# From mixing to the second feed-forward: token tiles in groups of four, norms of two tiles at once, no GpSimd

## The chip, the cores and the metric

The kernel runs on one core of a Trainium2 chip. The metric is the time of one execution on the device in microseconds (us); lower is better. Five engines work beside each other, each through its own queue in order: TensorE (PE) multiplies and transposes into the eight banks of PSUM, VectorE (DVE), ScalarE (ACT) and GpSimd (POOL) compute between SBUF and PSUM, and SyncE (SP) issues the DMAs. The engines wait for each other by semaphores.

## What is computed

One decoder layer on 1024 tokens of width 1024, fp32. A SwiGLU feed-forward, a mixing stage (sliding-window attention beside a diagonal state-space model), and a second SwiGLU feed-forward, each with a norm ahead and a norm behind, and with a shift, a scale and a gate from a conditioning vector:

```python
x = x + 0.5 * ga1 * rms_norm(swiglu(modulate(rms_norm(x, g_pre_ff1), sh1, sc1), ...), g_post_ff1)
h = modulate(rms_norm(x, g_pre_mix), sh2, sc2)
attn, ssm = sliding_window_attention(...), s5_ssm(...)     # both from h @ w_in
# the end of s5_ssm: y * sigmoid(y @ w_glu + b_glu)
mixed = concatenate([rms_norm(attn, g_attn_out), rms_norm(ssm, g_ssm_out)]) @ w_out
x = x + ga2 * rms_norm(mixed, g_post_mix)
h = modulate(rms_norm(x, g_pre_ff2), sh3, sc3)
x = x + 0.5 * ga3 * rms_norm((silu(h @ w2_gate) * (h @ w2_up)) @ w2_down, g_post_ff2)
```

The stage that is changed is the end of the second half: the GLU, the half of `mixed` that comes from `ssm`, the two norms around `x + ga2 * ...`, the modulation, and the first products of the second feed-forward.

## The kernel before

Each fp32 operand of a product is held as two halves: `split` (L68) lets ACT cast the high part (L69) and DVE or POOL subtract it to get the low part (L70). A product is three matmuls (`mm3`, L72): high by high (L74), high by low (L75), low by high (L76). Tokens are taken in eight tiles of 128. The feed-forwards use a scheme of Strassen's kind on halves of the tokens and of the width; `GateUp` holds its activations in eight buffers `q0` to `q7`, one for each 128 columns of the width, each with all 1024 tokens, and `Weights` its weights, whose raw halves are loaded into the buffers `r0` to `r3` of 512 KB.

Code is written in program order and a scheduler (the Tile framework) sets the order of each engine's queue from it; a buffer is named by its tag (`a14`, `c0`, `b6`), and whoever takes a tag again waits until its last readers are done. `b0` to `b7` are the PSUM banks.

The end of `mix`, by lines: the GLU (L1012 to L1030) makes the state-space half and adds up its squares (`sqs`, the add at L1030 on POOL). Then a loop runs over the token tiles t. It multiplies the tile by the lower half of `w_out` into two banks; for t = 0 it also sums the squares over the columns by eight matmuls with ones (L1054). DVE adds the banks, scaled, to `acc[t]` (L1058), which holds the attention's half. `epilogue` (L249) loads the tile's residual x, takes the squares' sum (ACT L156), multiplies by the gate (L254, here on POOL), forms 1/rms by a short chain of operations on 128x1 (L141 to L145, L151), adds the residual (DVE L255), stores x, takes the squares' sum again and normalises (ACT L259). `turn(t)`, called three tiles later, calls `to_hf` (L210): four transposes (L205) go into a bank, four more into a second one, and the blocks of 128x128 are scaled and shifted one at a time into the `q` buffers, four by ACT (L222) and four by DVE (L226). As soon as tiles 0 to 3 stand in `q0` to `q3`, `g2.block` splits these into operands and `g2.first` starts the gate and up products. `wt.first` splits the first raw weights; POOL forms the low part of four of these, and of two of the operands.

Of the eight `acc` tiles, those of tiles 0 to 2 lie in `r1` to `r3`, the others in `a14`, `a15`, `a4`, `a5`, `a6`. Earlier, at the end of the attention, `late` loads and splits the GLU weights by way of `r0` and `c0`.

## Time and profile before

| | us |
|---|---|
| runs | 1713.24, 1706.69, 1712.78 |
| median | 1712.78 |
| the profiled execution, its own time | 1704.67 |
| its span in the trace | 1702.9 |
| PE busy in it | 1649.9 |
| the stage in question (GLU to the first gate and up products) | about 970 to 1115 |

The profile is one execution, and the times of all rows are from it. "Busy" is the time in which an engine executes; matmuls overlap a little, so their durations add up to more than the time between their starts, and the distance from start to start is the one to count with. The bracket at the end of a row of a timeline gives how long the engine stood idle before it, and what the trace takes for the cause: engine, buffer and line of the last thing it waited for. Names are those of the buffers without their numbers: `a<-r,a` is an operation that reads buffers `r` and `a` and writes an `a`. The granted clock is the share of TensorE's full speed.

### The profile page before, as it was taken

To read this page: it belongs to the slowest core of one execution; us is meant where nothing else is said; L and a number is where in the kernel's file an instruction comes from. 1 tells how busy PE (TensorE), PEld (TensorE's weight loads), DVE (VectorE), ACT (ScalarE), POOL (GpSimd) and SP (SyncE) were. 2 spreads that over 40 slices of the span, in tenths; PEclk is the share of its full clock that TensorE was granted. 3 is DMA by queue.
4 is the path that set the end of the run, shared out by engine and by line. 5 is a ranking of instruction groups with operands and counts; after the bars stand their busy time and mean duration, and the time that the engine had idled before them with its cause. 6 is when DMAs were issued, how large, how long until landed. Compare 5 with 4: busy or idle time off the path is not lost.

```text
span 1702.9 us, 22218 instructions
## 1 busy us (share of the span) xinstructions
PE 1649.9 (97%) x7669; PEld 1353.3 (79%) x7669; DVE 1264.4 (74%) x2470; ACT 803.6 (47%) x1654; POOL 120.7 (7%) x147
## 2 busy tenths in 40 slices
PE   6999999999999999899989998999999999999998
PEld 5888888787788878788767886878888888888886
DVE  7999988789779878735589368777666566678586
ACT  5633333553344557736564257633333333444462
POOL 0011100001100000000014053000000000000001
PEclk8999999999999999999999998999999999999999
DMA  9186742234495733410233126253322223493324
GB/s 382 40 284 232 257 163 94 105 135 148 137 355 189 231 121 136 163 36 15 90 97 87 50 81 200 75 201 106 117 94 93 93 101 123 158 377 114 112 97 163
DMA packets 112066, 249.08 MB, mean 146 GB/s; under 512 B 12089, under 2 KB 27745, under 8 KB 111953
## 3 DMA queue, kind: packets, MB, share of 16 engines
q1 hardware_dynamic: 102224, 214.12, 36.6%
q0 software_dynamic: 9152, 32.49, 5.7%
q8 instruction: 60, 0.98, 0.2%
q10 hardware_dynamic: 576, 1.05, 0.2%
q14 instruction: 54, 0.43, 0.1%
HBM read 187.87 MB, written 59.75 MB: 145 GB/s over the span
## 4 chain that ended last, share of the span: by engine, by line
PE 50%; DVE 5%; ACT 2%; DMA 1%; issue 1%; SPq 0%; POOL 0%; DVEq 0%; ACTq 0%; POOLq 0%
PE b L76 15%; PE b L75 15%; PE b L74 15%; PE b L751 1%; PE b L839 1%; PE b L841 1%; DVE a L70 1%; PE b L840 1%; PE b L930 1%; PE b L785 1%; PE b L926 1%; ACT a L69 0%; PE b L205 0%; DMA r<-in_w_gu 0%; DMA w<-in_w_out 0%
## 5 line engine op out<-in xcount | busy, mean ns | idle before, releaser
L75 PE MATMUL b<-a,w 128*128 128x512 f32 x1260 | 493.5, 392 | 5.0 <-DVE a L70 5.0
L74 PE MATMUL b<-a,w 128*128 128x512 f32 x1260 | 489.2, 393 | 8.6 <-ACT w L69 3.5
L76 PE MATMUL b<-a,w 128*128 128x512 f32 x1260 | 494.2, 392 | 3.2 <-DVE w L70 3.1
L74 PEld LDWEIGHTS b<-a,w 128*128 128x128 f32 x1260 | 238.0, 189 | 61.6 <-ACT w L69 3.9
L76 PEld LDWEIGHTS b<-a,w 128*128 128x128 f32 x1260 | 238.3, 189 | 55.6 <-DVE w L70 5.9
L75 PEld LDWEIGHTS b<-a,w 128*128 128x128 f32 x1260 | 238.2, 189 | 55.1 <-DVE a L70 6.1
L70 DVE TENSOR_TENSOR w<-r,w 128x512 fp32r<-128x512 f32 (+1 forms) x206 | 142.9, 694 | 128.6 <-ACT w L69 128.3
L75 PE MATMUL b<-w,r 128*128 128x512 f32 x528 | 205.5, 389 | 1.7 <-DVE w L70 1.7
L76 PE MATMUL b<-w,r 128*128 128x512 f32 x528 | 205.4, 389 | 0.0
L74 PE MATMUL b<-w,r 128*128 128x512 f32 x528 | 180.7, 389 | 0.0
L69 ACT CAST w<-r 128x512 fp32r<-128x512 f32 (+1 forms) x210 | 130.2, 623 | 91.8 <-DVE r L334 82.1
L69 ACT CAST r<-a 128x512 fp32r<-128x512 f32 x110 | 68.5, 623 | 148.9 <-PE b L76 112.0
L70 DVE TENSOR_TENSOR r<-a,r 128x512 fp32r<-128x512 f32 x110 | 75.7, 688 | 60.3 <-ACT r L69 59.9
L75 PEld LDWEIGHTS b<-w,r 128*128 128x128 f32 x528 | 99.1, 188 | 22.7 <-DVE w L70 2.1
L76 PEld LDWEIGHTS b<-w,r 128*128 128x128 f32 x528 | 99.1, 188 | 20.6
L74 PEld LDWEIGHTS b<-w,r 128*128 128x128 f32 x528 | 99.1, 188 | 20.5
L69 ACT CAST w<-t 128x512 fp32r<-128x512 f32 (+1 forms) x114 | 69.9, 613 | 87.4 <-DVE t L337 33.5
L70 DVE TENSOR_TENSOR w<-t,w 128x512 fp32r<-128x512 f32 (+1 forms) x114 | 79.7, 699 | 32.4 <-ACT w L69 32.1
L466 DVE TENSOR_TENSOR h<-h,b 128x512 f32<-128x512 f32 x120 | 82.1, 685 | 20.4 <-PE b L76 18.6
L454 ACT ACTIVATE h<-h 128x512 f32<-128x512 f32 x60 | 38.0, 633 | 117.8 <-DVE h L466 117.8
L70 DVE TENSOR_TENSOR w<-a,w 128x512 fp32r<-128x512 f32 x110 | 75.4, 685 | 0.4 <-ACT w L69 0.4
L74 PE MATMUL b<-a,a 128*128 128x512 f32 x182 | 72.0, 398 | 0.0
(376 smaller groups left out, 2548.2 us busy)
## 6 DMA issues: line engine op xcount, KB each, us to landing
r<-in_w_gu SPq DMA_DIRECT2D x88, 512.0 KB, 4.1
g_d<-h SPq DMA_DIRECT2D x154, 256.0 KB, 2.2
a<-g_d SPq DMA_DIRECT2D x110, 256.0 KB, 3.4
q<-in_w_ada POOLq DMA_DIRECT2D x48, 512.0 KB, 4.6
a<-in_w_d SPq DMA_DIRECT2D x88, 256.0 KB, 5.4
a<-in_w_ada SPq DMA_DIRECT2D x16, 512.0 KB, 10.1
a<-in_x SPq DMA_DIRECT2D x12, 512.0 KB, 5.9
x_d<-a SPq DMA_DIRECT2D x12, 512.0 KB, 3.8
```

The lines of the kernel that those rows point to most:

```text
L69: act.copy(hi, src)
L70: eng.tensor_tensor(lo, src, hi.bitcast(F32), op=SUB)
L74: pe.matmul(psum, wh, xh, start=first, stop=False, skip_group_check=goes_on)
L75: pe.matmul(psum, wh, xl, start=False, stop=False, skip_group_check=goes_on)
L76: pe.matmul(psum, wl, xh, start=False, stop=last, skip_group_check=goes_on)
L454: act.activation(dst, src, AF.Silu)
L466: dve.tensor_tensor(dst, dst, pb, op=ADD)
L751: pe.matmul(pb[kv][:, m % 2, ks], qT[m][rows, t * P : (t + 1) * P], kT[rows, (t + 1 - nk) * P : (t + 1) * P], start=True, stop=True,)
L785: pe.transpose(pt[:, m, :], pr[4 * kv + m][:, b * P : (b + 1) * P], ident)
L839: pe.matmul(pb, hh, wh, start=k == 0, stop=False)
L840: pe.matmul(pb, hh, wl, start=False, stop=False)
L841: pe.matmul(pb, hl, wh, start=False, stop=k == NK - 1)
```

## The change

In words, in the order of the diff:

- `GateUp.first` is cut up, so that the products of one operand block can be called alone (`first_part`).
- Two of the GLU's raw weights are loaded into `a9` instead of `c0`, and `acc[4]` lies in `c0` instead of `a15`.
- The squares are added up by DVE. The low parts of weights and operands are formed by DVE as well, and so is the gate multiply. POOL computes nothing in this stage.
- The loop over tiles becomes three functions. `share(t)` multiplies, adds to `acc[t]`, lets ACT sum the squares in two halves and DVE multiply by the gate in place. `joined(p)` does the norms of tiles 2p and 2p + 1: one chain on 128x2 for both, the residuals, the stores, the squares, a second chain, the normalised tiles. `turn(c, k)` transposes columns k of the four tiles of group c into one bank and lets ACT scale and shift the whole bank, 128x512, at once.
- Their order is written out: three shares, pair 0, two shares, pair 1, two shares, pair 2, group 0 with its operands, the loads of the raw weights, share 7, the rest of group 0, pair 3, and group 1 between the products.
- Residuals are loaded into four buffers instead of two.

```diff
+        def first_part(self, r, c, k, us):
+            x = self.A[f"a{r + 1}{c + 1}"][k]
+            for u in us:
+                for f in range(2):
...
+                    w = self.wt.ops[u, f, c][:, :, k * P : (k + 1) * P]
+                    mm3(self.pb[r, u, f], w[:, 0], w[:, 1], x[:, 0], x[:, 1], c == 0 and k == 0, c == 1 and k == 3)
...
+                self.first_part(r, c, k, (0, 1))
...
-        return Stream(ins, Rot(*names("r", 2, 3, 0, 1)), 3), Stream(us, Rot("w2", "w3"), 1), Stream(late, Rot("a14", "a15", "a14", "a15", "r0", "c0", "r0", "c0"), 1), Stream(shares, Rot(*names("w", 0, 1, 2, 3)), 3)
+        return Stream(ins, Rot(*names("r", 2, 3, 0, 1)), 3), Stream(us, Rot("w2", "w3"), 1), Stream(late, Rot("a14", "a15", "a14", "a15", "r0", "a9", "r0", "a9"), 1), Stream(shares, Rot(*names("w", 0, 1, 2, 3)), 3)
...
-            acc.append(slot(("r1", "r2", "r3", "a14", "a15", "a4", "a5", "a6")[t], [D]))
+            acc.append(slot(("r1", "r2", "r3", "a14", "c0", "a4", "a5", "a6")[t], [D]))
...
-                    pool.tensor_tensor(sqs[:, tk], sqs[:, tk], s2, op=ADD)
+                    dve.tensor_tensor(sqs[:, tk], sqs[:, tk], s2, op=ADD)
...
-        x_rot = Rot("a10", "a11")
...
-        def turn(t):
-            to_hf(t, acc[t], hf, 2, 2)
...
-        for t in range(NT):
...
+        def share(t):
...
-            epilogue(1, t, acc[t], grow, x_rot(), "a13", ("c0", "a8")[t % 2], True, pool)
-            if t >= 3:
-                turn(t - 3)
-            if t == 3:
...
-                    wt.load(u, 0)
-            if t == 5:
...
-                    wt.load(u, 1)
-                wt.first(0)
-            if t >= 6:
-                for k in range(3) if t == 6 else (3,):
-                    g2.block(0, 0, k)
+            X[t] = slot(("a10", "a11", "a13", "a8")[t % 4], [D])
+            sp.dma_start(X[t], x_d[1][t])
...
+            for dh, (dk, pb) in enumerate(zip(halves, pbs)):
+                f = acc[t][:, dk]
+                dve.scalar_tensor_tensor(f, pb, rstd_s[:, t : t + 1], f, op0=MUL, op1=ADD)
+                i = 2 * dh + t % 2
+                act.activation(slot(j_rot(), [512]), f, AF.Square, accum_out=ss[:, i : i + 1])
+            dve.tensor_tensor(acc[t], acc[t], grow, op=MUL)
...
+        def joined(p):
...
+            ss, sn = S[p]
+            dve.tensor_tensor(ss[:, 0:2], ss[:, 0:2], ss[:, 2:4], op=ADD)
+            r = rstd_of(ss[:, 0:2], 2, D)
+            for i in range(2):
+                t = 2 * p + i
+                dve.scalar_tensor_tensor(X[t], acc[t], r[:, i : i + 1], X[t], op0=MUL, op1=ADD)
+                sp.dma_start(x_d[2][t], X[t])
+                act.activation(acc[t], X[t], AF.Square, accum_out=sn[:, i : i + 1])
+            r = rstd_of(sn, 2, D)
+            for i in range(2):
+                t = 2 * p + i
+                act.activation(acc[t], X[t], AF.Identity, scale=r[:, i : i + 1])
...
+        def turn(c, k):
...
+            pt = bank(tr_rot(), [4, P])
+            for i in range(4):
+                pe.transpose(pt[:, i, :], acc[4 * c + i][:, k * P : (k + 1) * P], ident)
+            act.activation(
+                g2.q(c, k // 4, k % 4), pt.rearrange("p t q -> p (t q)"), AF.Identity,
+                scale=gsc[:, 2, k : k + 1], bias=mod(6)[:, k : k + 1],
+            )
...
+        for t in range(4):
+            share(t)
+            if t == 2:
+                joined(0)
+        share(4)
+        joined(1)
+        share(5)
+        share(6)
+        joined(2)
+        for k in range(4):
+            turn(0, k)
+            g2.block(0, 0, k)
+        for c in range(2):
+            for u in range(2):
+                wt.load(u, c)
+        wt.first(0)
+        share(7)
+        for k in range(4, 8):
+            turn(0, k)
...
-        g2.first(0, 0, lambda k: turn({0: 5, 2: 6}[k]) if k % 2 == 0 else None)
...
+            g2.first_part(0, 0, k, (0, 1))
+        joined(3)
...
-        g2.first(0, 1, lambda k: turn(7) if k == 1 else None)
+        g2.first(0, 1, lambda k: [turn(1, 2 * k + i) for i in range(2)])
...
-        return GateUp(2, Weights(a["w2_gu"], names("a", 16, 17, 18, 19), pool), hf, {
+        return GateUp(2, Weights(a["w2_gu"], names("a", 16, 17, 18, 19), dve), hf, {
...
-            "s2": names("a", 0, 1, 2, 3), "s3": names("a", 16, 17, 18, 19)}, pool)
+            "s2": names("a", 0, 1, 2, 3), "s3": names("a", 16, 17, 18, 19)}, dve)
```

What the scheduler makes of it is seen at three places. In these rows a name carries its buffer and the number of the tile that lies in it, and a bracket names the semaphores that the instruction waits on. Lines of the changed kernel are its own: L1089 is the transpose in `turn`, L1090 its eviction, L1079 the second squares and L1083 the normalised tile in `joined`.

PE at the seam, before: the last transposes (tiles 3 and 4), then the first products of the second feed-forward.

```order
L205 MATMUL b6_1620_9355<-ident_69,a14_1423_8424 128x128 [waits DVE_49,Activation_49]
L205 MATMUL b6_1620_9355<-ident_69,a14_1423_8424 128x128 x3
L205 MATMUL b7_1619_9346<-ident_69,a14_1423_8424 128x128 [waits Activation_49]
L205 MATMUL b7_1619_9346<-ident_69,a14_1423_8424 128x128 x3
L205 MATMUL b6_1638_9440<-ident_69,a15_1431_8494 128x128 [waits DVE_49,Activation_49]
L205 MATMUL b6_1638_9440<-ident_69,a15_1431_8494 128x128 x3
L205 MATMUL b7_1637_9431<-ident_69,a15_1431_8494 128x128 [waits Activation_49]
L205 MATMUL b7_1637_9431<-ident_69,a15_1431_8494 128x128 x3
L74 MATMUL b0_1640_9452<-a7_1621_9364,w0_1602_9276 128x512 [waits Activation_49]
```

Each tile fills two banks with four blocks each, and the first product follows the last transposes at once.

PE at the same place, after, from the last columns of group 0 on:

```order
L1089 MATMUL b6_1599_9309<-ident_69,r1_1405_8288 128x128 [waits Activation_49]
L1089 MATMUL b6_1599_9309<-ident_69,r2_1408_8317 128x128
L1089 MATMUL b6_1599_9309<-ident_69,r3_1420_8395 128x128
L1089 MATMUL b6_1599_9309<-ident_69,a14_1423_8424 128x128
L1089 MATMUL b7_1618_9430<-ident_69,c0_1431_8494 128x128 [waits Activation_49]
L1089 MATMUL b7_1618_9430<-ident_69,a4_1434_8523 128x128
L74 MATMUL b0_1601_9318<-a14_1580_9224,w0_1587_9244 128x512 [waits Activation_49]
L74 MATMUL b1_1602_9322<-a14_1580_9224,w1_1588_9247 128x512
L1089 MATMUL b6_1619_9436<-ident_69,c0_1431_8494 128x128 [waits PE_49,Activation_49]
L1089 MATMUL b6_1619_9436<-ident_69,a4_1434_8523 128x128
L75 MATMUL b0_1601_9318<-a14_1580_9224,w0_1587_9244 128x512 [waits DVE_49]
```

The transposes of four tiles share a bank now, and behind those of group 0 stand two each of tiles 4 and 5 (`c0`, `a4`), ahead of and between the matmuls with the operand a14.

ACT at the seam, before, from the evictions of tile 3 on:

```order
L222 ACTIVATE q0_1502_8839<-b7_1619_9346,modc_77,gsc_78 128x128 [waits PE_49]
L222 ACTIVATE q1_1503_8840<-b7_1619_9346,modc_77,gsc_78 128x128
L222 ACTIVATE q2_1504_8841<-b7_1619_9346,modc_77,gsc_78 128x128
L222 ACTIVATE q3_1505_8842<-b7_1619_9346,modc_77,gsc_78 128x128
L69 CAST a20_1648_9540<-q4_1506_8843 128x512 [waits DVE_49]
L69 CAST a21_1649_9543<-q5_1507_8844 128x512 [waits DVE_49]
L69 CAST a22_1650_9546<-q6_1508_8845 128x512 [waits DVE_49]
L69 CAST a7_1621_9364<-q0_1502_8839 128x512 [waits Activation_49]
L69 CAST a23_1651_9549<-q7_1509_8846 128x512 [waits DVE_49]
L69 CAST a9_1622_9367<-q1_1503_8840 128x512 [waits Activation_49]
L69 CAST a14_1623_9370<-q2_1504_8841 128x512 [waits Activation_49]
```

Here no norm of a tile stands between the evictions and the casts.

ACT at the same place, after:

```order
L1090 ACTIVATE q4_1506_8843<-b7_1596_9291,modc_77,gsc_78 128x512 [waits PE_49]
L141 ACTIVATE s1609_9382<-s1608_9380 128x2 [waits DVE_49]
L1090 ACTIVATE q5_1507_8844<-b6_1597_9297,modc_77,gsc_78 128x512 [waits PE_49]
L69 CAST a20_1600_9315<-q4_1506_8843 128x512 [waits Activation_49]
L1083 ACTIVATE c0_1431_8494<-a10_1546_9063,s1574_9192 128x1024 [waits DVE_49]
L1083 ACTIVATE a4_1434_8523<-a11_1559_9127,s1574_9192 128x1024
L1090 ACTIVATE q6_1508_8845<-b7_1598_9303,modc_77,gsc_78 128x512 [waits DMAHW2_49,PE_49]
L69 CAST a21_1605_9334<-q5_1507_8844 128x512 [waits Activation_49]
L69 CAST a14_1580_9224<-q2_1504_8841 128x512 [waits PE_49]
L1090 ACTIVATE q7_1509_8846<-b6_1599_9309,modc_77,gsc_78 128x512 [waits DMAHW2_49]
L1079 ACTIVATE a5_1437_8552,s1566_9165<-a13_1564_9162 128x1024 [waits DVE_49]
L1079 ACTIVATE a6_1440_8581,s1566_9165<-a8_1593_9282 128x1024 [waits DVE_49]
```

The evictions cover 128x512, and two normalised tiles (L1083, tiles 4 and 5) stand between the evictions of q5 and q6, ahead of the cast of a14.

DVE at the end of the attention, before (L914 and L915 form the operand of L930; the row with `c0` splits GLU weights):

```order
L913 TENSOR_TENSOR a4_1278_7683<-a4_1278_7683,q3_1282_7687 128x512 [waits DVE_49]
L70 TENSOR_TENSOR h7_1455_8633<-c0_1453_8630,h6_1454_8632 128x512 [waits DMAHW5_49,Activation_49]
L914 TENSOR_TENSOR a5_1279_7684<-a5_1279_7684,q3_1282_7687 128x512 [waits DVE_49]
L897 TENSOR_TENSOR a4_1278_7683<-b5_1391_8159,q2_1358_8062 128x512 [waits DVE_49,DMAHW3_49,PE_49,Pool_49]
L915 TENSOR_TENSOR a9_1334_7945<-a4_1278_7683,a5_1279_7684 128x4x127 [waits DVE_49]
```

The split is the row between the halves of the same sum, L913 and L914.

DVE at the same place, after (L916 to L918 are L913 to L915):

```order
L916 TENSOR_TENSOR a4_1278_7683<-a4_1278_7683,q3_1282_7687 128x512 [waits DVE_49]
L917 TENSOR_TENSOR a5_1279_7684<-a5_1279_7684,q3_1282_7687 128x512 [waits DVE_49]
L900 TENSOR_TENSOR a4_1278_7683<-b5_1391_8159,q2_1358_8062 128x512 [waits DVE_49,DMAHW3_49,PE_49,Pool_49]
L918 TENSOR_TENSOR a9_1334_7945<-a4_1278_7683,a5_1279_7684 128x4x127 [waits DVE_49]
L902 TENSOR_TENSOR a5_1279_7684<-b5_1391_8159,q2_1358_8062 128x512 [waits DVE_49]
```

The split is gone from here.

And where it stands now, among the copies of the attention's half into the `acc` tiles (L961):

```order
L70 TENSOR_TENSOR q3_1444_8611<-a12_1276_7681,q1_1443_8610 128x1024 [waits Activation_49,Pool_49]
L961 TENSOR_SCALAR a14_1423_8424<-b6_1424_8425,rstd_a_81 128x512 [waits PE_49]
L961 TENSOR_SCALAR a14_1423_8424<-b7_1425_8439,rstd_a_81 128x512 [waits PE_49]
L70 TENSOR_TENSOR h7_1455_8633<-a9_1453_8630,h6_1454_8632 128x512 [waits DMAHW3_49,Activation_49]
L961 TENSOR_SCALAR c0_1431_8494<-b4_1432_8495,rstd_a_81 128x512 [waits PE_49]
```

The split of the GLU weights has moved from ahead of L914 to behind the copies into a14.

## Rows read from the trace of the kernel before

**Rows 1.** Page, busy time of each engine, share of the span, instructions.
```profile
PE 1649.9 (97%) x7669; PEld 1353.3 (79%) x7669; DVE 1264.4 (74%) x2470; ACT 803.6 (47%) x1654; POOL 120.7 (7%) x147
```

**Rows 2.** Stretches: length, busy PE, PEld, DVE, ACT, POOL, granted clock, DMA share, GB/s.
```profile
1000.00:1020.00 20.00, 19.52 (x85) 15.90 (x85) 13.12 (x32) 7.46 (x14) 8.47 (x4) 0.91 0.07 27
...
1040.00:1060.00 20.00, 12.22 (x47) 8.84 (x46) 18.98 (x44) 15.83 (x36) 8.17 (x4) 0.74 0.54 184
```

**Rows 3.** Timeline of PE, statistics: start, duration, operation, [idle before <- releaser].
```profile
1000.88 0.40 PE L74 MATMUL b<-a,a 128*128 128x512 f32 x1
1001.76 1.05 PE L1054 MATMUL b<-ones,a 128*128 128x1 f32 x8 [0.48 <-POOL a L1030]
...
1003.51 0.63 PE L75 MATMUL b<-a,a 128*128 128x512 f32 x1
...
1007.10 0.39 PE L75 MATMUL b<-a,a 128*128 128x512 f32 x1
1007.33 0.40 PE L76 MATMUL b<-a,a 128*128 128x512 f32 x1
```

**Rows 4.** Timeline of PE, the seam into the second feed-forward.
```profile
1042.26 0.60 PE L205 MATMUL b<-ident,a 128*128 128x128 f32 x4
1043.06 0.66 PE L205 MATMUL b<-ident,a 128*128 128x128 f32 x4 [0.20 <-ACT q L222]
1047.22 0.63 PE L205 MATMUL b<-ident,a 128*128 128x128 f32 x4 [3.50 <-ACT a L69]
1049.20 1.11 PE L205 MATMUL b<-ident,a 128*128 128x128 f32 x4 [1.35 <-ACT q L222]
1051.26 2.08 PE L74 MATMUL b<-a,w 128*128 128x512 f32 x4 [0.94 <-ACT a L69]
1055.12 0.79 PE L75 MATMUL b<-a,w 128*128 128x512 f32 x1 [1.79 <-DVE a L70]
...
1058.38 1.07 PE L74 MATMUL b<-a,w 128*128 128x512 f32 x4
```

**Rows 5.** Timeline of DVE, single operations between 1011 and 1053 us.
```profile
1011.73 0.16 DVE L144 TENSOR_TENSOR s<-s,s 128x1 f32<-128x1 f32 x1
...
1012.67 1.27 DVE L255 SCALAR_TENSOR_TENSOR a<-c,s,a 128x1024 f32<-128x1024 f32 x1
...
1043.64 0.69 DVE L70 TENSOR_TENSOR a<-r,a 128x512 fp32r<-128x512 f32 x1
...
1046.66 0.40 DVE L226 TENSOR_SCALAR q<-b,gsc,modc 128x128 f32<-128x128 f32 x1
...
1052.16 2.30 DVE L255 SCALAR_TENSOR_TENSOR a<-a,s,a 128x1024 f32<-128x1024 f32 x1
```

**Rows 6.** Timeline of PE, end of the attention.
```profile
905.59 0.49 PE L930 MATMUL b<-q,a 64*128 64x128 f32 x4 [1.31 <-DVE a L915]
```

**Rows 7.** Timeline of DVE, the same place.
```profile
900.90 1.77 DVE L70 TENSOR_TENSOR h<-c,h 128x512 fp32r<-128x512 f32 x1
```

**Rows 8.** Timeline of POOL, two subtractions of 128x512.
```profile
1029.41 2.53 POOL L70 TENSOR_TENSOR w<-r,w 128x512 fp32r<-128x512 f32 x2
```

**Rows 9.** Timeline of ACT, single operations between 979 and 1044 us.
```profile
979.78 0.68 ACT L1022 ACTIVATE t<-b,cols 128x512 f32<-128x512 f32 x1
980.37 1.14 ACT L671 ACTIVATE a<-w,cols 128x1024 fp32r<-128x1024 f32 x1
...
1024.21 1.48 ACT L222 ACTIVATE q<-b,modc,gsc 128x128 f32<-128x128 f32 x4
...
1038.39 1.16 ACT L259 ACTIVATE a<-a,s 128x1024 f32<-128x1024 f32 x1 [1.30 <-DVE s L144]
...
1042.99 1.14 ACT L69 CAST a<-r 128x512 fp32r<-128x512 f32 x2
```

**Rows 10.** DMA issues, 960 to 1100 us: count, KB each, median us to landing.
```profile
r<-in_w_gu SPq DMA_DIRECT2D x8, 512.0 KB, 3.8
```

**Rows 11.** Timeline of PE, behind the seam.
```profile
1108.80 0.50 PE L76 MATMUL b<-a,w 128*128 128x512 f32 x1 [0.81 <-DVE w L70]
```

More of the change, by code (lines that the diff above doesn't have):

```diff
@@ L394, in s34 @@
                 self.put("s4", k, self.q(0, 1, k))
+        def first_part(self, r, c, k, us):
+            x = self.A[f"a{r + 1}{c + 1}"][k]
+            for u in us:
+                for f in range(2):
+                    if c == 0 and k == 0:
+                        self.pb[r, u, f] = bank(f"b{4 * r + 2 * u + f}")
+                    w = self.wt.ops[u, f, c][:, :, k * P : (k + 1) * P]
+                    mm3(self.pb[r, u, f], w[:, 0], w[:, 1], x[:, 0], x[:, 1], c == 0 and k == 0, c == 1 and k == 3)
         def first(self, r, c, between=None):
             for k in range(4):
-                x = self.A[f"a{r + 1}{c + 1}"][k]
-                for u in range(2):
-                    for f in range(2):
-                        if c == 0 and k == 0:
-                            self.pb[r, u, f] = bank(f"b{4 * r + 2 * u + f}")
-                        w = self.wt.ops[u, f, c][:, :, k * P : (k + 1) * P]
-                        mm3(self.pb[r, u, f], w[:, 0], w[:, 1], x[:, 0], x[:, 1], c == 0 and k == 0, c == 1 and k == 3)
+                self.first_part(r, c, k, (0, 1))
                 if between:
@@ L1038, in mix @@
         wt = g2.wt
-        x_rot = Rot("a10", "a11")
-        def turn(t):
-            to_hf(t, acc[t], hf, 2, 2)
-        for t in range(NT):
+        halves = slice(0, 512), slice(512, D)
+        j_rot = Rot(*names("h", 4, 5, 6, 7))
+        X, S = {}, {}
+        def share(t):
             tk = slice(t * P, (t + 1) * P)
             pbs = [bank(f"b{(2 * t + dh) % 6}") for dh in range(2)]
-            for dh, pb in enumerate(pbs):
-                dk = slice(dh * 512, dh * 512 + 512)
+            for dk, pb in zip(halves, pbs):
                 for m in range(4):
@@ L1055, in mix @@
                 dve.tensor_copy(rstd_s, rstd_of(pc, 8, 512))
-            for dh, pb in enumerate(pbs):
-                dk = slice(dh * 512, dh * 512 + 512)
-                dve.scalar_tensor_tensor(acc[t][:, dk], pb, rstd_s[:, t : t + 1], acc[t][:, dk], op0=MUL, op1=ADD)
-            epilogue(1, t, acc[t], grow, x_rot(), "a13", ("c0", "a8")[t % 2], True, pool)
-            if t >= 3:
-                turn(t - 3)
-            if t == 3:
-                for u in range(2):
-                    wt.load(u, 0)
@@ L1065, in mix @@
-            if t == 5:
-                for u in range(2):
-                    wt.load(u, 1)
-                wt.first(0)
-            if t >= 6:
-                for k in range(3) if t == 6 else (3,):
-                    g2.block(0, 0, k)
+            X[t] = slot(("a10", "a11", "a13", "a8")[t % 4], [D])
+            sp.dma_start(X[t], x_d[1][t])
+            if t % 2 == 0:
+                S[t // 2] = small(4, "ssm2"), small(2, "ssn2")
+            ss = S[t // 2][0]
+            for dh, (dk, pb) in enumerate(zip(halves, pbs)):
[3 more added lines that the diff above has]
+                act.activation(slot(j_rot(), [512]), f, AF.Square, accum_out=ss[:, i : i + 1])
```

## The prediction

> **What bounds the kernel now.** The table of busy time comes first: TensorE (PE) works 1649.9 of the span's 1702.9 us, 97% [rows 1]. Work taken from another engine is therefore worth nothing in itself; to be won is only time in which PE stands, or runs at less than its full clock. The table of stretches shows where that is in the stage that the change touches [rows 2]: from 1000 to 1020 us PE is busy 19.52 us at granted clock 0.91, from 1040 to 1060 us for 12.22 us at 0.74, while DVE is busy 18.98 us, ACT 15.83 and POOL 8.17. PE's timeline of these stretches and of the end of the attention gives three losses.
>
> Loss A, the statistics [rows 3]. Eight one-column matmuls (L1054) wait for POOL's last sum of squares (L1030). From 1000.88 to 1007.10 us, 6.22 us, 13 matmuls of 512 columns run and these eight. At full clock such matmuls follow each other by 0.23 us (1007.10, 1007.33), and the eight take 1.05. So 6.22 - 13 x 0.23 - 1.05 = 2.2 us are lost: 0.65 to the wait (1001.76 - 1000.88 - 0.23), and the rest, 1.55, to some eight matmuls from 1003.51 on that take 0.63 instead of 0.40 (1000.88), the lower clock after a stretch in which PE had little to do: 0.2 for each.
>
> Loss B, the seam [rows 4]. From 1042.26 to 1058.38 us, 16.12 us, PE does 16 transposes (0.60 for the first four, 0.15 each) and 12 matmuls. 16.12 - 2.4 - 2.8 = 10.9 us are lost: 0.20 + 3.50 + 1.35 + 0.94 + 1.79 = 7.8 to five waits, the rest to the lower clock. The 3.50 before 1047.22 is put down to an ACT cast, but what came last is on DVE: the bank's last block (L226) ends at 1046.66 + 0.40 = 1047.06 [rows 5]. The last wait, 1.79, is for a lo half that DVE forms behind a residual of 2.30 us (1052.16); the same operation took 1.27 at 1012.67 [rows 5]. A likely reason for the difference is that POOL works beside the longer one.
>
> Loss C [rows 6, 7]: at 905.59 us PE waits 1.31 us for DVE's L915. Ahead of that on DVE stands, at 900.90, a split of the GLU weights (h<-c,h) of 1.77 us.
>
> **The change part by part.** *Statistics.* The six adds go from POOL (1.27 each: two subtractions of that shape take 2.53 [rows 8]) to DVE (0.69 [rows 5]). The last one ends 0.6 us sooner and the wait of 0.65 goes. DVE has room (13.12 of 20 us [rows 2]). Whether the clock still falls no row shows: the narrow matmuls stay. So 0.65 to 2.2; I take the middle, **1.4**.
>
> *Seam.* ACT now evicts a chunk of 128x512 at once. Nearest row: an activation of that shape out of PSUM, at 979.78, 0.68, whose last 0.09 lie beside the next one at 980.37: 0.59 [rows 9]. Taken in the same way, four blocks cost 1.38 (1024.21), on ACT and as much again on DVE, a cast 0.52 (two in 1.14, 1042.99), a normalised tile 1.06 (1038.39) [rows 9]. By the order of the changed program ACT does between the eviction of q4 and the cast a14 on which the next matmul waits: three evictions, a root of two columns (0.1, by the 0.16 of DVE's narrow operations [rows 5]), three casts, and two normalised tiles of the next group: 1.77 + 0.10 + 1.56 + 2.12 = 5.55 us. PE has 14 transposes for that time, 2.1 us, of which 0.6 may lie ahead of it: a hole of 3.5 to 4.0, I take 3.8, and 0.3 for DVE's lo half behind it, 4.1. The scheduler has pulled the transposes of tiles 4 and 5 ahead of these matmuls; they are why two normalised tiles stand in ACT's way. Then comes w2: ACT needs 0.59 + 2 x 1.06 + 0.52 = 3.2 us until its cast, PE has 12 matmuls and two transposes, 3.06: up to 0.4, I take 0.3. Lower clock after the hole: none to all 12 matmuls at 0.2 more, 2.4; I take 1.6, eight slow ones as in loss A. That makes 6.0 us lost, where 10.9 were. Bounds: 3.5 + 0.3 = 3.8 below; above, 4.0 + 0.3 + 0.4 + 2.4 = 7.1, and 2 more if the raw weights come late: they go into the buffers of tiles 0 to 2, so their loads start after the last transposes of these, land 3.8 us later [rows 10], and 2 of those lie behind ACT's own queue; 9.1. Gain **4.9**, from 1.8 to 7.1.
>
> *GLU weights in another buffer.* The split leaves the row ahead of L914 and stands in the changed order behind the last copy into a14, among the L961. 1.67 us less ahead of L915 is more than the wait of 1.31. The split's 0.69 may return among the L961. From 0.6 to 1.3; I take **0.8**.
>
> *Loads of the engines.* DVE takes from POOL 6 sums and 6 lo halves at 0.69 and 8 gate multiplies at the 1.27 of the residual, which has the same shape: 18.4 us. It gives up 32 blocks L226 (by ACT's row 8 x 1.38 = 11.0), 36 of 80 operations on norms (0.16 each, 1011.73 [rows 5], 5.8), and what POOL's work beside it may cost, by the residual 2.30 - 1.27 = 1.0. 18.4 against 17.8: about even. ACT gets 16 evictions and 16 half squares at 0.59, 18.9; it gives up 32 blocks (8 x 1.38) and 8 squares at the 1.06 of a normalised tile, 19.5: even. PE has the same matmuls and 64 transposes as before. New waits that follow from it: ACT's in-order queue now holds a pair's normalised tiles behind a DVE chain, and behind them evictions for PE; that is priced above. The x loads now have four buffers in place of two and come earlier beside PE's shares: nothing. What changes later, behind 1100 us, is bounded by the wait of 0.81 there [rows 11]: 0, give or take 0.8.
>
> *Sum:* 1.4 + 4.9 + 0.8 = 7.1 us; bounds 0.65 + 1.8 + 0.6 - 0.8 = 2.3 and 2.2 + 7.1 + 1.3 + 0.8 = 11.4. Against the profiled execution: span 1702.9 to 1695.8, its time 1704.67 to 1697.6. The median of the runs, 1712.78, lies 8.1 above that execution; on it the gain gives **1705.7**. About 0.5%, 8.5 us, is what a measurement of this kernel can tell from no change.
>
> **The rivals.** *1. The clock does not fall* (chance 0.26). Without the POOL wait PE stays at full clock in the statistics, and the seam's hole is too short to lower it: 2.2 + 7.1 + 1.3 = 10.6, **1702.2**. For it: the short wait of 0.20 before 1043.06 leaves the four transposes behind it nearly as long as the four before, 0.66 to 0.60. Against it: 0.65 us of waiting with eight narrow matmuls was enough at 1001.76.
>
> *2. Groups of four give the gain back* (0.15). Chunks of four tiles can't start until the fourth is normalised, where before each tile was turned when ready. If ACT runs the two squares of the following pair (2 x 1.06) in front of a14's cast too, all 12 matmuls come at the lower clock (0.8 more) and the raw weights are late (2.0), B loses 6.0 + 2.1 + 0.8 + 2.0 = 10.9 as before; then A gives 0.65 and C 0.6: **1711.5**. For it: in the seam ACT is already busy 15.83 of 20 us. Against it: the order puts those squares behind the cast. The Trainium skill's page "Perfetto Trace Analysis", section "Optimizing Scalar/DVE Operations", speaks for this rival: where these engines aren't saturated but make others wait, it says, breaking instructions up may let work finish sooner, and this change does the opposite. By that rule the sum would be that of this rival; the trace of before is mixed, since DVE is nearly saturated at the seam and ACT is not.
>
> *3. DVE becomes the bound* (0.09), on the other side. It takes 14.3 us of POOL's work in this stage (18.4 without the six sums). If the longer residual has nothing to do with POOL, and the L226 blocks were hidden beside ACT's, only the 5.8 of small operations and 1.0 us free at the seam stand against that: 7.5 us more on PE's path, and 1.6 for eight more matmuls at low clock: **1721.9**. It decides if DVE's work at the seam grows by more than it has free. Against it: the bank that PE waited longest for was emptied last by L226.
>
> *4. The change doesn't do what it says*: that the order of the program takes tiles 4 and 5 ahead of the matmuls is in the forecast; in all else it follows the code.
>
> **How the numbers follow.** Forecast 0.50, of it 0.18 beyond 1704.2, which is 0.5% below the median; rival 1 0.26; rival 2 0.15; rival 3 0.09. Faster 0.18 + 0.26 = 0.44; within 0.5% 0.32 + 0.15 = 0.47; slower 0.09. The range reaches from 1697, what the forecast gives for a run like the profiled one (1697.6), through rivals 1 and 2 to 1712, and leaves rival 3 out.
>
> **What would show it.** Right: no POOL in the stage; L1056's matmuls without a wait; at the seam one PE wait of 3.5 to 4.3 us before the first matmul on a14, with two L1083 on ACT in it, and matmuls 0.43 apart behind it; no wait of 1.3 before L930's counterpart. Wrong: a wait for a raw weight of over 2 us, a chunk's transposes waiting for L1083 before the shares are through, or DVE full from 1000 to 1060 us with PE waiting for it.

## The result and the profile after

The changed kernel takes 1699.62 us in the median of eight runs (1696.87 to 1703.8), the kernel before 1710.7 in eight (1706.69 to 1716.64). The ratio is 0.9941, with a 95% interval from 0.9924 to 0.9959: about 10 us faster, between 7 and 13. The profiled execution took 1701.33 us, its span is 1699.5.

The stretches of the profile after that answer to [rows 2], in the same columns (busy PE, PEld, DVE, ACT, POOL, granted clock, DMA share, GB/s):

```profile
1000.00:1020.00 20.00, 20.00 (x98) 16.80 (x97) 13.52 (x27) 8.39 (x20) 0.00 (x0) 1.00 0.09 27
...
1040.00:1060.00 20.00, 16.35 (x72) 12.44 (x72) 14.99 (x32) 18.93 (x37) 0.00 (x0) 0.83 0.58 188
```

The statistics run at full clock now, and POOL does nothing. At the seam PE is busy 16.35 us instead of 12.22. DVE has 5 of 20 us free; ACT is the full engine, with 18.93.

How much the stage changed is read off two rows of PE's timeline that both kernels have: the first product of the GLU, and the first product of the second feed-forward's down projection, far behind the seam. Before and after:

```profile
970.05 0.39 PE L74 MATMUL b<-q,h 128*128 128x512 f32 x1
...
1483.02 0.61 PE L74 MATMUL b<-w,r 128*128 128x512 f32 x2
```

```profile
973.77 0.39 PE L74 MATMUL b<-q,h 128*128 128x512 f32 x1
...
1479.64 0.62 PE L74 MATMUL b<-w,r 128*128 128x512 f32 x2
```

That is 512.97 us before and 505.87 after, 7.10 less. The GLU itself starts 3.7 us later: set against the kernel before, this execution was 5.1 us behind near the end of the attention, in code that the change leaves alone, and had 1.4 of them back by the GLU (the last section tells how such a lag comes about). For that reason the spans of the two profiles, 3.4 us apart, say less than this stretch, and every kernel below is measured by it.

At the seam, the timeline of PE after:

```profile
1043.54 0.50 PE L75 MATMUL b<-a,w 128*128 128x512 f32 x1 [0.17 <-DVE a L70]
...
1047.42 0.55 PE L1089 MATMUL b<-ident,r 128*128 128x128 f32 x3 [0.43 <-ACT q L1090]
...
1051.44 0.47 PE L1089 MATMUL b<-ident,c 128*128 128x128 f32 x1 [2.60 <-ACT q L1090]
...
1052.47 1.22 PE L74 MATMUL b<-a,w 128*128 128x512 f32 x2 [0.34 <-ACT a L69]
...
1055.62 0.63 PE L74 MATMUL b<-a,w 128*128 128x512 f32 x1
...
1057.52 0.39 PE L74 MATMUL b<-a,w 128*128 128x512 f32 x1
```

And ACT in the same time:

```profile
1046.59 0.78 ACT L1090 ACTIVATE q<-b,modc,gsc 128x512 f32<-128x512 f32 x1 [0.46 <-PE b L1089]
1047.26 0.19 ACT L141 ACTIVATE s<-s 128x2 f32<-128x2 f32 x1
1047.36 0.77 ACT L1090 ACTIVATE q<-b,modc,gsc 128x512 f32<-128x512 f32 x1
1048.02 0.61 ACT L69 CAST a<-q 128x512 fp32r<-128x512 f32 x1
1048.53 1.15 ACT L1083 ACTIVATE c<-a,s 128x1024 f32<-128x1024 f32 x1
1049.58 1.14 ACT L1083 ACTIVATE a<-a,s 128x1024 f32<-128x1024 f32 x1
1050.62 0.77 ACT L1090 ACTIVATE q<-b,modc,gsc 128x512 f32<-128x512 f32 x1
1051.28 1.13 ACT L69 CAST a<-q 128x512 fp32r<-128x512 f32 x2
```

Where five waits of 7.8 us stood in [rows 4], there are four of 3.5. The long one, 2.60, stands ahead of the transposes of tiles 4 and 5. It ends 0.05 us behind the eviction that starts at 1050.62 and empties a bank for them; ahead of that eviction ACT normalises these two tiles (L1083), which takes 2.1 us. These transposes in turn stand ahead of the product on a14. From the first of these evictions to the cast of a14 ACT takes 5.7 us (from 1046.59 to 1052.31, where its next operation starts). Behind the hole eight matmuls are slow: six take 0.63, and two, each behind a pause or a transpose, about 0.8.

### The profile page after: what moved, and what is told of

Read it like the earlier page. It is cut to its first block, busy times and chain, and to the rows that moved or that the text cites. A ratio compares the mean times of both kernels' runs of the same rounds, so it can differ in the third digit from the quotient of the medians.

```text
span 1699.5 us, 22120 instructions
## 1 busy us (share of the span) xinstructions
PE 1650.8 (97%) x7669; PEld 1354.1 (80%) x7669; DVE 1254.7 (74%) x2422; ACT 803.9 (47%) x1646; POOL 82.2 (5%) x127
## 3 DMA queue, kind: packets, MB, share of 16 engines
q10 hardware_dynamic: 576, 1.05, 0.2%
## 4 chain that ended last, share of the span: by engine, by line
PE 53%; DVE 4%; DMA 1%; ACT 1%; issue 1%; SPq 0%; DVEq 0%; ACTq 0%
PE b L74 15%; PE b L76 15%; PE b L75 15%; PE b L754 1%; PE b L842 1%; PE b L844 1%; PE b L843 1%; PE b L933 1%; DVE a L70 1%; PE b L788 1%; PE b L929 1%; PE b L891 0%; DMA x_d<-q 0%; DVE h L432 0%; DVE a L764 0%
## 5 line engine op out<-in xcount | busy, mean ns | idle before, releaser
L69 ACT CAST w<-a 128x512 fp32r<-128x512 f32 x110 | 67.8, 616 | 8.5 <-PE b L76 6.2
```

The lines of the kernel that those rows point to most:

```text
L69: act.copy(hi, src)
```

## The experiments

The stretch from the GLU to the down projection, in us, and the ratio of the time to that of the kernel before:

| kernel | stretch | ratio, 95% interval |
|---|---|---|
| before; a second execution | 512.97; 514.39 | 1 |
| before, sums on DVE | 510.47 | one run |
| before, GLU weights in a9 | 511.23 | 0.9986 (0.9972 to 1.0000) |
| before, no POOL in the stage | 509.10 | 0.9987 (0.9967 to 1.0006) |
| changed, all POOL work back on POOL | 514.61 | 0.9977 (0.9956 to 0.9998) |
| changed; a second execution | 505.87; 505.63 | 0.9941; 0.9934 (0.9906 to 0.9962) |
| changed, sums on POOL | 506.82 | 0.9950 (0.9933 to 0.9968) |
| changed, tiles 4 and 5 normalised later | 505.66 | 0.9948 (0.9929 to 0.9967) |
| changed, four banks | 501.93 | 0.9922 (0.9904 to 0.9939) |
| changed, four banks, two operands swapped, half of the evictions on DVE | 499.23 | 0.9888 (0.9864 to 0.9911) |

A stretch is that of one execution, and the kernel before alone differs by 1.4 us in it; a ratio is that of several executions of the whole kernel, and its interval is 5 to 10 us wide. Two kernels that differ by one line can also differ in more than that line does, since the scheduler orders the queues anew.

**What one execution says.** Both kernels were traced a second time, unchanged.

> The changed kernel once more, for a second execution in the trace. Theory (what differs between executions of one kernel is for how long the clock stays lowered around 700 and 885 us and behind the statistics, while the waits at the seam are the kernel's own): the waits at the seam come again within 0.2 us, 3.5 in all; the stretch from GLU to the down product is 505.9 within 1, the start of GLU may lie several us elsewhere. Rival: the waits at the seam differ by 1 us or more, so that one trace says little on them.

> The kernel before once more, for a second execution in the trace. Theory: 7.8 us of waits at the seam again, within 0.5; behind the statistics the matmuls take 0.63 or 0.40 by chance, so that the stretch from GLU to the down product is 511.2 to 513.0. Rival: the lower clock behind the statistics belongs to the wait for POOL and comes each time, 513.0 within 0.4.

The changed kernel nearly repeated itself: 0.17, 0.43, 2.60 and 0.59 us of waits at the seam, 3.8 together, the last 0.25 longer than before, and 505.63 in all. The kernel before had the same five waits (0.40, 3.50, 0.86, 0.94, 1.79, together 7.5), but more matmuls at the lower clock behind them, and came to 514.39, outside what was expected. The slow matmuls behind its statistics came again, so the expectation that they come by chance rests on the next kernels.

**The sums of squares.** In the changed kernel the add goes back to POOL, and in the kernel before it goes to DVE:

```diff
-                    dve.tensor_tensor(sqs[:, tk], sqs[:, tk], s2, op=ADD)
+                    pool.tensor_tensor(sqs[:, tk], sqs[:, tk], s2, op=ADD)
```

> The changed kernel with one edit: the sums of squares go back to POOL. Theory (the gain at the statistics is POOL's late last sum): PE waits about 0.5 us for the second set of narrow matmuls, some eight matmuls behind it take 0.63 instead of 0.40, and the stretch from the first GLU matmul to the first down product of the second feed-forward, 505.87 us in the changed kernel's profile and 512.97 before, becomes 0.65 to 2.2 longer. Rival (the gain there came from the narrow matmuls standing further apart, with POOL without a part): no wait, no slow matmuls, 505.9 within 0.4.

> The kernel before with only the sums of squares on DVE. Theory: the wait for POOL ahead of the narrow matmuls goes, and with it the slow matmuls behind it that came in two of three executions of the kernel with c0 or a9: no 0.63 there, GLU to down product 510.5 to 511.5 (two executions of before: 512.97 and 514.39, the latter with more slow time at the seam). Rival: PE still falls to the lower clock behind the narrow matmuls, which are there as before: 512.3 or more.

PE's timeline of the changed kernel with its sums on POOL:

```profile
1004.11 1.05 PE L1056 MATMUL b<-ones,a 128*128 128x1 f32 x8 [1.04 <-POOL a L1033]
1005.02 0.48 PE L75 MATMUL b<-a,a 128*128 128x512 f32 x1
1005.34 0.40 PE L76 MATMUL b<-a,a 128*128 128x512 f32 x1
```

The wait is back, 1.04 us, and the stretch is 1.0 to 1.2 longer; but nothing behind it is slow. The statistics by themselves take 1.5 longer. The seam gives some of that back: its queues come in another order here, with five waits, the longest 1.11, in place of the one of 2.60. The kernel before with its sums on DVE has no wait there and no slow matmul, 510.47:

```profile
1004.90 0.94 PE L1054 MATMUL b<-ones,a 128*128 128x1 f32 x8
```

So the wait is POOL's, worth 0.7 to 1.5 us (0.7 where the kernel with the GLU weights in a9, below, has it). The slow matmuls behind it came in two of five executions that had the wait (both of the kernel before), and in none of the seven without it.

**The GLU weights in a9**, in the kernel before:

```diff
-        return Stream(ins, Rot(*names("r", 2, 3, 0, 1)), 3), Stream(us, Rot("w2", "w3"), 1), Stream(late, Rot("a14", "a15", "a14", "a15", "r0", "c0", "r0", "c0"), 1), Stream(shares, Rot(*names("w", 0, 1, 2, 3)), 3)
+        return Stream(ins, Rot(*names("r", 2, 3, 0, 1)), 3), Stream(us, Rot("w2", "w3"), 1), Stream(late, Rot("a14", "a15", "a14", "a15", "r0", "a9", "r0", "a9"), 1), Stream(shares, Rot(*names("w", 0, 1, 2, 3)), 3)
```

> The kernel before with one edit: the GLU's raw weights are loaded into a9 instead of c0, so their split moves from ahead of the attention's sums to behind the copies. Theory: the wait of 1.31 us ahead of L930 at the end of the attention goes, 0.6 to 1.3 us less, and the time lies 0.0 to 0.1% below that of before. Rival (the split's place costs as much as it frees, or the wait is set by POOL working beside DVE): a wait of the same size stays there or elsewhere among the last attention blocks, no gain.

The wait of [rows 6] is gone. The transposes ahead of that place and the first matmul behind it, before and with this edit:

```profile
903.79 0.49 PE L926 MATMUL b<-q,a 128*128 128x128 f32 x2
905.59 0.49 PE L930 MATMUL b<-q,a 64*128 64x128 f32 x4 [1.31 <-DVE a L915]
```

```profile
904.32 0.49 PE L926 MATMUL b<-q,a 128*128 128x128 f32 x2
904.74 0.49 PE L930 MATMUL b<-q,a 64*128 64x128 f32 x4
```

At the transposes PE lies 0.53 us later than in the trace of before, at the matmul 0.85 earlier: 1.4 us won, a little more than expected. What the wait costs without the edit is not the same in each execution: it is 1.97 in the second one of before, 0.89 with the sums on DVE, and none in the kernel before without POOL, where PE came 11.9 us later to it after a long spell of the lower clock. The edit lies ahead of the stretch in the table, and the 511.23 there is not its work: this execution waited 0.39 us for POOL at the statistics, without slow matmuls behind it. The ratio, 0.9986, is some 2 us, with nothing just inside its interval.

**POOL and grouping taken apart.** The kernel before without POOL, and the changed kernel with all of POOL's work given back to it. Each has the line of the sums as above besides, and the second the two lines of `GateUp` with POOL:

```diff
-            epilogue(1, t, acc[t], grow, x_rot(), "a13", ("c0", "a8")[t % 2], True, pool)
+            epilogue(1, t, acc[t], grow, x_rot(), "a13", ("c0", "a8")[t % 2], True, dve)
...
-        return GateUp(2, Weights(a["w2_gu"], names("a", 16, 17, 18, 19), pool), hf, {
+        return GateUp(2, Weights(a["w2_gu"], names("a", 16, 17, 18, 19), dve), hf, {
```

```diff
-            dve.tensor_tensor(acc[t], acc[t], grow, op=MUL)
+            pool.tensor_tensor(acc[t], acc[t], grow, op=MUL)
```

> The kernel before with one edit: all that POOL computes in this stage (sums, gate multiplies, low parts) goes to DVE; tiles, norms and evictions stay single. Theory (grouping is what makes room for POOL's work on DVE): the statistics gain their 2 us, but DVE gets 14.3 us more in the stage where it is busy 18.98 of 20 us at the seam, PE waits there longer, and the stretch from GLU to the down product is 0 to 6 us longer than the 512.97 of before. Rival (taking POOL out is the whole gain, since DVE's work is stretched by POOL): 507 or less, as in the changed kernel.

> The changed kernel with POOL's work given back to POOL (sums, gate multiplies, low parts); groups, pairs, order and buffers stay. With the kernel before, the kernel before without POOL (GLU to down product 509.1) and the changed kernel (505.87 and 505.63) this makes a square. Theory (both parts are worth something: POOL's late sum and its work beside DVE about 2 to 3 us, grouping about 3 to 4): 508 to 510, POOL's multiplies beside longer DVE operations, and PE's wait for POOL at the statistics back. Rival (grouping alone brings all at the seam, POOL only the wait at the statistics): 506.5 to 507.2.

Neither expectation held. Without POOL the kernel before gains some 4 us of the stretch, though DVE got POOL's work; with POOL the changed kernel has lost all of its gain in the stretch, 514.61. The times are milder. By its ratio the first gains some 2 us (from 6 less to 1 more), and the second still gains 4 (0.3 to 7.5), of which the GLU weights, which it keeps, may be one. They show that the kernel without grouping falls short of the changed one: the intervals do not meet, and the 8 us between the two ratios are more than the GLU weights are worth. With POOL back the intervals overlap by a hair. In the profiled execution with POOL back, its DVE and POOL, and the waits that follow on PE and ACT:

```profile
1046.04 2.45 DVE L70 TENSOR_TENSOR a<-q,a 128x512 fp32r<-128x512 f32 x1 [1.62 <-ACT a L69]
...
1050.11 2.26 DVE L145 SCALAR_TENSOR_TENSOR s<-s,s 128x2 f32<-128x2 f32 x1
```

```profile
1045.58 2.36 POOL L1068 TENSOR_TENSOR a<-a,a 128x1024 f32<-128x1024 f32 x1 [6.97 <-ACT h L1067]
1049.99 2.36 POOL L1068 TENSOR_TENSOR a<-a,a 128x1024 f32<-128x1024 f32 x1 [2.04 <-ACT h L1067]
```

```profile
1048.55 0.79 PE L75 MATMUL b<-a,w 128*128 128x512 f32 x1 [1.26 <-DVE a L70]
...
1055.31 0.55 PE L1089 MATMUL b<-ident,r 128*128 128x128 f32 x3 [1.34 <-ACT q L1090]
```

```profile
1052.40 1.15 ACT L1083 ACTIVATE c<-a,s 128x1024 f32<-128x1024 f32 x1 [1.99 <-DVE s L145]
```

A DVE subtraction that takes 0.69 elsewhere takes 2.45 and ends half a microsecond behind POOL's multiply, and an operation on two columns takes 2.26 for 0.16. PE waits for the first of them. ACT waits 1.99 us for the second, and the eviction for which PE waits 1.34 stands behind that in its queue. The kernel before has the same: four operations of its norms on 128x1 take 0.92 to 1.96 us in this stage for 0.16, and each ends within 0.02 us of an operation of POOL. One of them, with POOL's row:

```profile
1009.74 1.96 DVE L143 SCALAR_TENSOR_TENSOR s<-s 128x1 f32<-128x1 f32 x1
```

```profile
1009.29 2.39 POOL L254 TENSOR_TENSOR a<-r,a 128x1024 f32<-128x1024 f32 x1 [1.07 <-DVE s L151]
```

In the stage of the changed kernel and of the kernel before without POOL no such operation takes over 0.3. Working in pairs makes one more kind sensitive. The scaling at the head of a norm (L151) takes 0.15 on 128x1 in the kernel before, also when POOL is at work, as from 1014.75 to 1017.15. On 128x2, with POOL back, it takes 1.24 to 2.33 in all four places where it starts beside POOL, and ends within 0.03 us of POOL each time. The kernel before, then the changed one with POOL back:

```profile
1015.22 0.15 DVE L151 TENSOR_SCALAR s<-s 128x1 f32<-128x1 f32 x1 [0.61 <-ACT r L156]
```

```profile
1036.37 2.27 DVE L151 TENSOR_SCALAR s<-s 128x2 f32<-128x2 f32 x1
```

That grouping is worth so little beside POOL may come from this; PE has no wait between 1006 and 1043 us in that execution, so it is not shown. The Trainium skill's page "SBUF — State Buffer", section "Who interferes with whom", has a reason: a DVE instruction with two inputs in SBUF contends with a GpSimd instruction that reads SBUF, over a pair of ports that is held exclusively. The rows agree for the two operations shown first, 2.45 and 2.26 us beside multiplies of 2.36. So it is not the count of DVE's operations alone that matters at the seam, but whether POOL stands in the middle of one that another engine needs. How much of the 8.7 us that this stretch is longer than the changed kernel's is due to that is not shown: the queues of this kernel come in another order too, and its slow matmuls are 21 against eight.

In the kernel before without POOL, PE's one long wait at the seam is 5.39 us, for the cast of the first operand. ACT has the cause in its queue: the second raw weight, for which it waits 1.02 us, four evictions, and the squares of two tiles, all ahead of that cast:

```profile
1052.00 1.14 ACT L69 CAST a<-r 128x512 fp32r<-128x512 f32 x2 [1.02 <-DMA r<-in_w_gu]
1053.05 1.50 ACT L222 ACTIVATE q<-b,modc,gsc 128x128 f32<-128x128 f32 x4
1054.43 1.06 ACT L156 ACTIVATE a<-a 128x1024 f32<-128x1024 f32 x1
...
1055.46 1.06 ACT L156 ACTIVATE a<-a 128x1024 f32<-128x1024 f32 x1
...
1056.50 1.66 ACT L69 CAST a<-q 128x512 fp32r<-128x512 f32 x3
```

**The hole in the changed kernel.** First the two normalised tiles are tied behind the last eviction of group 0:

```diff
+                if prev is not None:
+                    tc.add_manual_dep(
+                        nc.cur_bb.bb.instructions[-1], prev.name,
+                        mybir.DependencyInfo(mybir.DependencyClass.NoSync, mybir.DependencyReason.DATA), reason="late",
+                    )
...
-        joined(2)
...
+        joined(2, nc.cur_bb.bb.instructions[-1])
```

> The changed kernel with one edit: the two normalised tiles of pair 2 (L1083) are tied behind the last eviction of group 0, so that they no longer stand on ACT between the evictions of q5 and q6. Theory (these 2.1 us in ACT's queue make the hole in PE): the wait of 2.60 us ahead of the transposes of tile 4 goes, in all about 1.3 us of waits are left ahead of the first product on a14, and the stretch from GLU to the down product is 1.0 to 2.3 us shorter than 505.87; more is not to be had, since the cast of w2 (ended 2.3 us before PE needed it) stays where it was. Rival (ACT's whole queue up to w2 is the bound, 18.93 of 20 us busy): the wait turns up again in front of w2 or of the next tiles, 505.9 within 0.4.

PE's timeline of this kernel:

```profile
1055.74 0.55 PE L1094 MATMUL b<-ident,r 128*128 128x128 f32 x3 [0.43 <-ACT q L1095]
...
1058.71 1.22 PE L74 MATMUL b<-a,w 128*128 128x512 f32 x2 [1.55 <-ACT a L69]
1060.43 0.69 PE L1094 MATMUL b<-ident,c 128*128 128x128 f32 x2 [0.50 <-ACT c L1083]
...
1064.52 0.63 PE L75 MATMUL b<-a,w 128*128 128x512 f32 x1
...
1065.52 0.47 PE L74 MATMUL b<-a,w 128*128 128x512 f32 x1
```

From the wait of 0.43 to the first product on a14 pass 2.97 us, where 5.05 passed in the changed kernel (1047.42 to 1052.47): the two tiles, with two transposes that now come later, were 2.08 of the hole. The waits left ahead of that product are 1.98, where 1.3 were expected. And from that product to the first one on w2 (1065.52) pass 6.81, where 5.05 passed (1057.52): 1.76 are given back, 0.50 of it to a new wait for L1083 among these products, most of the rest to matmuls at the lower clock, twelve where there were eight. The stretch is 505.66, what the rival gave; of the way that it named, a wait in front of the next tiles, only the 0.50 came.

Then the transposes rotate through four banks:

```diff
+        t_rot = Rot("b6", "b7", "b4", "b5")
...
-            pt = bank(tr_rot(), [4, P])
+            pt = bank(t_rot(), [4, P])
```

> The changed kernel with one edit: the transposes of four tiles rotate through four PSUM banks (b6, b7, b4, b5, the latter two free at the seam) instead of two. By its order all 16 transposes of the last columns of group 0 then stand in a row, the cast of a14 comes two evictions later, and the normalised tiles of pair 2 behind the weights. Theory (PE and ACT take turns over two banks, and a14's buffer is released only by the last of these transposes): less than 1 us of waits is left at the seam, no matmul there takes 0.63, and the stretch from the first GLU matmul to the first down product of the second feed-forward is 3 to 5 us shorter than the changed kernel's 505.87. Rival (ACT's work as a whole sets the end of the seam): the waits turn up at w2 or at the next operands (a20 to a23), and the stretch is at most 1 us shorter.

PE's timeline of this kernel, from the last columns of group 0 on:

```profile
1041.64 0.49 PE L1090 MATMUL b<-ident,r 128*128 128x128 f32 x3
...
1043.31 0.71 PE L74 MATMUL b<-a,w 128*128 128x512 f32 x2
...
1047.15 0.73 PE L74 MATMUL b<-a,w 128*128 128x512 f32 x2 [0.85 <-ACT a L69]
1047.90 0.50 PE L75 MATMUL b<-a,w 128*128 128x512 f32 x1
1048.24 0.39 PE L76 MATMUL b<-a,w 128*128 128x512 f32 x1
```

Sixteen transposes stand in a row, without a wait; one wait of 0.85 is left, and no matmul behind it is slow. The stretch falls by 3.7 to 3.9 us, as the theory had it. The hole was thus the exchange of PE and ACT over two banks, with ACT's work in the middle of it, and the lower clock came with it. By the order that follows from the edit the two normalised tiles move behind the weights too; moved alone, above, they gave nothing, and banks alone were not tried. Last, what was left:

```diff
-            "a11": names("a", 7, 9, 14, 15), "a12": names("a", 20, 21, 22, 23), "a21": names("a", 24, 25, 26, 27),
+            "a11": names("a", 7, 9, 15, 14), "a12": names("a", 20, 21, 22, 23), "a21": names("a", 24, 25, 26, 27),
...
+            if k % 2 == 1:
+                dve.tensor_scalar(dst, src, gsc[:, 2, k : k + 1], mod(6)[:, k : k + 1], op0=MUL, op1=ADD)
+            else:
+                act.activation(dst, src, AF.Identity, scale=gsc[:, 2, k : k + 1], bias=mod(6)[:, k : k + 1])
```

> The kernel with four banks and two edits more: a14 and a15 change places among the operands of the first products, so that the buffer that is released last is wanted last, and odd columns k are evicted by DVE. Theory (what is left at the seam, 0.85 us ahead of a14, is ACT's queue and a14's release): that wait falls below 0.5 us, the waits of 1.05 and 1.01 us behind it shrink by half, and GLU to down product is 0.5 to 1.5 us below the 501.93 of the kernel with four banks. Rival (DVE becomes the one that is waited for, since it evicts and splits in one queue): the sum of the waits stays, 501.9 within 0.5.

The stretch of the seam in its profile:

```profile
1040.00:1060.00 20.00, 20.00 (x100) 16.49 (x99) 19.90 (x37) 16.47 (x31) 0.00 (x0) 1.00 0.65 220
```

PE is busy all 20 us at full clock, beside a DVE that is now busy for 19.90 of them. The waits behind it are 0.30 and 0.91 for 1.05 and 1.01, so the second did not shrink by half as expected. With 499.23 the stretch is 2.7 us shorter still, more than expected; which of the two edits brought it was not taken apart. The kernel takes 1692.98 us in the median of six runs: 1.1% less than the kernel before, and the fastest of all.

## Why the prediction was right, and where it was off

The forecast was 7.1 us of gain and 1705.7 us; measured are some 10 us (7 to 13) and 1699.62, which lies inside the range from 1697 to 1712, on the faster side of the forecast and of the first rival (1702.2). That it lies inside owes something to luck. The prediction's own largest gain, 11.4 us, ends at 1701.4 on its median of 1712.78; the range went down to 1697 only to allow for executions as quick as the profiled one, and with five more runs the median before became 1710.7. The gain itself, some 10 us, lies within the bounds of 2.3 and 11.4.

- *Statistics, forecast 1.4 (0.65 to 2.2).* In the pair of profiles this gave 2.3: the place lies 3.72 us later than before ahead of it and 1.38 behind it. The wait went, as said. The upper bound was reached, since the slow matmuls went as well, but by the experiments these belong to the wait only at times. The wait alone is 0.7 to 1.5.
- *Seam, forecast 4.9.* It gave 4.8 (1.38 later to 3.38 earlier). Its working held in the parts: ACT took 5.7 us for the 5.55 reckoned (an eviction 0.67 instead of 0.59), PE's waits were 0.43 + 2.60 + 0.34 = 3.4 for 3.8, in three pieces where one was named, and eight slow matmuls came, as reckoned. The 0.3 for w2 didn't come. By the prediction's own count, the 10.9 us from 1045.94 to 1056.83 with 20 transposes and nine matmuls hold 5.8 us of loss; 6.0 were forecast. (That count takes 0.15 for a transpose, its busy time; from start to start it is some 0.1, by the sixteen from 1041.64 to 1043.31 in the kernel with four banks. It is so on both sides of the change.)
- *GLU weights, forecast 0.8 (0.6 to 1.3).* The wait went and PE won 1.4 there: in the profile after, the same two rows as above lie 5.14 us later than before ahead of the place (908.93) and 3.76 behind it (909.35). The split cost nothing where it stands now, which the forecast had left open.
- *Behind the seam, forecast 0 give or take 0.8.* The 4.8 of the seam is read up to the down projection and so holds this term. The waits near 1110 us make nearly the same sum, 0.81 and 0.68 before and 1.56 after.
- *The step that was mis-sized* is the one from the engines' loads. The sum counted POOL's leaving as nothing at the seam (18.4 us against 17.8) and put all of the gain to grouping. In the stretches of the four kernels grouping with POOL is worth nothing (514.61), leaving POOL out without grouping some 4 us, both together 7 to 9; by the ratios each half is worth something between nothing and most of the whole. So the share of each stays open, and what is shown is that without grouping the full gain does not come. What POOL costs DVE was in the trace of before: the residual of 2.30 beside POOL in [rows 5], from which the prediction took 1.0 us, and the four operations on norms of 0.92 to 1.96, 4.7 us more than the 0.16 at which it priced each.
- *The median.* The parts in the profiles make 2.3 + 4.8 + 1.4 = 8.5 us, inside the measured interval. The profiled execution of before was the quickest of its nine, which is why its span makes the gain look small.
- *The rivals.* The first (the clock does not fall) held at the statistics and not at the seam, where the clock granted was 0.83. The second did not come: ACT's hole was as long as reckoned. The rule on breaking instructions up that the prediction cited for it, from the Trainium skill's page "Perfetto Trace Analysis", section "Optimizing Scalar/DVE Operations", would have given the sum of this rival. The seam lost 4.8 us less, with larger evictions and without POOL together, and no run here changes the size of the evictions alone. The third did not come: without POOL DVE was busy for 14.99 of 20 us at the seam in the changed kernel, where it was 18.98 before.

## What to carry to other kernels

Look at what stands between the evictions of an in-order engine, and at how many banks two engines exchange over: two more banks let the transposes run ahead and removed a hole that moving ACT's work did not. A hole can cost twice, once as a wait and once as slow matmuls behind it, so one that is only shortened may give nothing back. And before work is taken from GpSimd or given to it, look for DVE operations, however small, that run longer beside it and that another engine waits for.

## What was not expected of the hardware

Executions of code that is the same in these kernels differ by several us, in good part through how long PE stays at the lower of its two clocks. In the kernel with tiles 4 and 5 normalised later, PE's matmuls of the attention were slow from 885 to 912 us; in the changed kernel with sums on POOL they were at full clock again from 891 on. Their stretches from 900 to 920 us, in this order:

```profile
900.00:920.00 20.00, 20.00 (x122) 15.42 (x122) 11.88 (x17) 10.25 (x21) 4.64 (x7) 0.71 0.27 80
```

```profile
900.00:920.00 20.00, 20.00 (x163) 15.51 (x161) 19.97 (x24) 12.65 (x25) 7.76 (x11) 1.00 0.55 146
```

PE is busy for all 20 us in both, with 122 instructions at 0.71 and 163 at 1.00. At 857 us of the kernel before the first lay 4.7 us behind that kernel and the second 2.7; by the GLU it was 12.0 and 1.6. What decides it stays open: the waits in front, near 882 us, make nearly the same sum in both, 4.1 and 3.9 us.

And the clock doesn't follow the sum of the waits. At the seam of the changed kernel with sums on POOL PE waited five times, 4.1 us together, the longest 1.11, and no matmul was slow; in the changed kernel 3.5 us, of which 2.60 in one piece, were followed by slow ones.
